# A longer hand-written order for ScalarE and VectorE through the gates of an mLSTM layer

## The chip, the cores and the metric

One Trainium2 chip, one of its cores. The metric is device time in microseconds (us) of one execution of the whole program; lower is better. TensorE multiplies matrices, ScalarE and VectorE work elementwise, GpSimd does small elementwise work, SyncE issues most of the transfers.

## The reference, cut to what matters

A decoder of two layers on 256 positions of width 1024, all in float32: an mLSTM mixer, a convolutional feed-forward net, an attention mixer and another feed-forward net. The change touches the mLSTM mixer:

```python
u = rmsnorm(x, norm_g) @ w_in
q, k, v, o, gi, gf = split(u)            # 4 heads; q, k 128 wide, v, o 256 wide
i_pre, f_pre = gi + b_gates[0], gf + b_gates[1]
lf = log_sigmoid(f_pre)                  # summed over the positions
...
s = (q @ k.T) * exp(decay)               # decay from the sums of lf, i_pre and a running maximum
h = s @ v / max(abs(sum(s)), exp(-m))
h = rmsnorm(h, h_norm_g) * sigmoid(o)
out = h @ w_out
```

## The kernel before, in words

Positions lie in two tiles of 128. TensorE does float32 products out of two rounded parts: every operand X is held as hi (X rounded, float32r) and lo (X minus hi). A weight *unit* is 128 x 2048 floats (1 MB): `unit` (L137) loads it into one of three `raw` buffers and splits it in two halves of 128 x 1024; for each half ScalarE writes hi (L144) and VectorE lo (L145), into one of four hi and four lo buffers.

The mLSTM layer (L429 to L634) has these stages for TensorE, in a written order that the change nearly keeps:

1. Gates (L525) and k, q (`kq_steps`, L516, products on L216 and L220): eight results kq0 to kq7 of 128 x 256, from units kq0 to kq3 of `w_kq`. Each result is evicted by `whole` (L253): a ScalarE copy (L257) and a VectorE addition (L258).
2. Among the steps of kq4 to kq7: the norm's sums (L185, L187, GpSimd L189 gives `rc`); `gates` (L453): two small products (L457), then VectorE L460 and L463, ScalarE Exp (L464), a table load and Ln (L465), VectorE `lf` (L466), the logarithm of the forget gate; `r.row` (L191) makes the row factor `rB` (L194, L196); `scale` (L520) multiplies each kq by `rB` (L521).
3. `sums_f` (L468): three small products with `lf` (L470 to L472), ScalarE `fc` (L473), GpSimd `av` (L474). Then four blocks of 16 steps over units vo0 to vo7 of `w_vo`, two units for each block; a step is three products of 512 columns (L237 to L239).
4. Block 1 (vo0, vo1): its results go to V (L572, L573); `maxima` (L476): transposes of `av`, VectorE L480, eight steps of a running maximum (L484), and the split into `mh`, `ml` (L488, by L150 and L151).
5. Block 2 (vo2, vo3): among its steps `decay` for four heads (products L500, L501 of `selr` with `mh` and `ml`; VectorE L503, L505; ScalarE Exp L507 into E), `floors` (transposes L493, VectorE L494 into `em`), and `scores` (L554, L555, then VectorE L556). These small results share three PSUM buffers named mis.

`mix(steps, items)` (L70) puts items among the steps by a running cost. TensorE's order is as written everywhere. For ScalarE and VectorE the order is as written only from L374 to `first.close()` on L544; from there a scheduler orders them by its own estimate of times, and units of weights that the written part does not hold back are placed where the scheduler finds an engine free. What a written instruction waits for holds up all that stands behind it on its engine.

Of the kernel before, what the change touches and what calls it, by code (L numbers as in the profile page):

```python
# [11 lines left out]
F32 = mybir.dt.float32  # L12
F32R = mybir.dt.float32r
BF16 = mybir.dt.bfloat16
AF = mybir.ActivationFunctionType
OP = mybir.AluOpType
AX = mybir.AxisListType

P = 128
# [6 lines left out]
MH = 4  # L26
# [43 lines left out]
def mix(steps, items=()):  # L70

    items, now = list(items), 0.0
    for cost, step in steps:
        while items and items[0][0] <= now:
            items.pop(0)[1]()
        step()
        now += cost
    for _, item in items:
        item()
# [3 lines left out]
def yoco_kernel(ctx: ExitStack, tc: tile.TileContext, A, out):  # L83
    nc = tc.nc
# [5 lines left out]
    wraw = ctx.enter_context(tc.tile_pool(name="wraw", bufs=3))  # L90
    wsp = ctx.enter_context(tc.tile_pool(name="wsp", bufs=4))
# [19 lines left out]
    for j in range(4):  # L111
        c = slice(j * 512, (j + 1) * 512)
# [24 lines left out]
    def unit(src, length, pieces=PIECES):  # L137
        raw = wraw.tile([P, 2048], F32, name="raw")[:, :length]
        nc.sync.dma_start(raw, src)
        hi = wsp.tile([P, 2048], F32R, name="hi")[:, :length]  # L140
        lo = wsp.tile([P, 2048], F32R, name="lo")[:, :length]
        for j in range(pieces):
            c = slice(j * length // pieces, (j + 1) * length // pieces)
            nc.scalar.activation(hi[:, c], raw[:, c], AF.Copy)  # L144
            nc.vector.tensor_tensor(lo[:, c], raw[:, c], hi[:, c].bitcast(F32), OP.subtract)  # L145
        return hi, lo

    def split(hi, lo, src, g=None):
        if g is None:
            nc.scalar.activation(hi, src, AF.Copy)  # L150
            nc.vector.tensor_tensor(lo, src, hi.bitcast(F32), OP.subtract)  # L151
        else:
            nc.scalar.activation(hi, src, AF.Copy, scale=g)
            nc.vector.scalar_tensor_tensor(lo, src, g, hi.bitcast(F32), op0=OP.mult, op1=OP.subtract)

# [84 lines left out]

        return [(0.64, lambda k=k: one(k)) for k in range(KD)]

    def block_x(src, first, x, done):

        u = [Once(lambda j=j: unit(src[first + j], 2048)) for j in range(2)]
        return [s for t in range(NT) for s in steps_x(t, u, x, done)]

    def acc():  # L250
# [122 lines left out]
    first = ExitStack()  # L373
# [55 lines left out]
    with tc.tile_pool(name="mls", bufs=1, reuse_waits="tile") as mp, \  # L429
# [1 line left out]
        r = Rstd()  # L431

        psg = acc()
        grow = []
        lf = mp.tile([P, NT, MH], F32, name="lf")
        gs = mp.tile([P, NT, 2 * MH], F32, name="gs")
        fc = mp.tile([P, NT, MH], F32, name="fc")
# [13 lines left out]
        E = [mp.tile([P, 384], F32, name=f"E{h}") for h in range(MH)]  # L451

        def gates():  # L453
            tc.keep_in_program_order(nc.scalar.activation(selr, sel, AF.Copy))
            pt = mis()
            for t in range(NT):
                nc.tensor.matmul(pt[:, t * 2 * MH:(t + 1) * 2 * MH], grow[0][:, t * P:(t + 1) * P], both8,  # L457
                                 start=True, stop=True)
            for t in range(NT):
                nc.vector.scalar_tensor_tensor(gs[:, t], pt[:, t * 2 * MH:(t + 1) * 2 * MH], r.rc[:, t:t + 1],  # L460
                                               row[:, R_G:R_G + 2 * MH], op0=OP.mult, op1=OP.add)
            fg = gs[:, :, MH:]
            nc.vector.scalar_tensor_tensor(lf, fg, -1.0, fg, op0=OP.mult, op1=OP.min)  # L463
            nc.scalar.activation(lf, lf, AF.Exp)  # L464
            nc.scalar.activation(lf, lf, AF.Ln, bias=1.0)  # L465
            nc.vector.scalar_tensor_tensor(lf, fg, 0.0, lf, op0=OP.min, op1=OP.subtract)  # L466

        def sums_f():  # L468
            pf = mis()
# [6 lines left out]
        def maxima():  # L476
            pa = mis()
            for t in range(NT):
                nc.tensor.transpose(pa[:MH, t * P:(t + 1) * P], av[:, t], ident)
            nc.vector.tensor_scalar(mx[0][:, P:], pa[:MH, :S], 0.0, None, op0=OP.max)  # L480
            src = 0
            for step in range(8):
                d = 1 << step
                nc.vector.tensor_tensor(mx[1 - src][:, P:], mx[src][:, P:],  # L484
                                        mx[src][:, P - d:P + S - d], OP.max)
                src = 1 - src

            split(mh[:MH], ml[:MH], mrow[:MH])  # L488

        def floors():  # L490
            pc = mis()
# [24 lines left out]
        def kq_steps(j):  # L516
            return steps_w(pk[j], wk[j // 2], lambda k: k * 256 + (j % 2) * P, setA, range(KD), KD,
                           lambda p: whole(p, kq[j]))

        def scale(j):  # L520
            nc.vector.tensor_tensor(kq[j], kq[j], r.rB, OP.mult)  # L521
# [17 lines left out]
        for k in range(3, KD):  # L539
            squares(k, nc.vector)  # L540
        mix(kq_steps(2)[1:] + kq_steps(3))
        mix([s for j in range(4, 2 * MH) for s in kq_steps(j)],
            [(2.3, r.sums), (2.4, wk[3]), (6.2, gates), (6.2, r.row), (10.0, sums_f)])
        first.close()  # L544
        for j in range(2 * MH):
            scale(j)


        PT = [[mp.tile([P, 384], F32R, name=f"PT{h}{j}") for j in range(2)] for h in range(MH)]
# [74 lines left out]
        def at(t0, dt, fn, args):  # L624
            return [(t0 + dt * i, lambda a=a: fn(*a)) for i, a in enumerate(args)]

        mix(block_x(A["w_vo"], 0, setA, v_done(0)), [(1.2, maxima)])
        nc.sync.dma_start(rope, A["rope"])
        mix(block_x(A["w_vo"], 2, setA, v_done(1)),
            at(1.8, 0.6, decay, [(h,) for h in range(MH)]) + [(4.2, floors)]  # L630
            + at(5.1, 1.2, scores, [(h,) for h in range(MH)]))
        mix(block_x(A["w_vo"], 4, setA, o_done(0)), at(0.9, 1.05, head, [(h, t) for h in range(MH) for t in range(NT)]))
# [202 lines left out]
```

## Time and profile before

| | us |
|---|---|
| median of 3 runs | 602.84 (601.43 to 603.41) |
| the profiled execution, its own time | 602.72 |
| its span in the trace | 601.0 |
| TensorE busy | 592.1 (99%) |
| VectorE, ScalarE, GpSimd busy | 484.8, 390.0, 159.2 |
| HBM read | 104.15 MB |

Times in the trace count from the start of the span; the program's own time is 1.7 us longer than the span. "Granted clock" is the share of TensorE's full clock that it was given: 1.0 is 2.4 GHz, 0.5 is 1.2 GHz. A row of a timeline with x6 is six instructions that follow each other; its length runs from the first one's start to the last one's end. A matmul is shown from its start to the end of its last column, which overlaps the next one, so the distance of two starts is its price in a stream.

### The profile page before, as it was taken

How to read it: one execution, taken by the hardware profiler on the slowest of the kernel's cores; microseconds unless marked ns; L12 is line 12 of the kernel's file. 1: busy time of each engine (PE TensorE's matmuls, PEld its weight loads, DVE VectorE, ACT ScalarE, POOL GpSimd, SP SyncE). 2: the span in 40 equal slices, each digit the busy share in tenths (PEclk: the TensorE clock that was granted, in tenths of full speed). 3: DMA queues.
4: the chain of work that ended last, by engine and by line, in shares of the span. 5: the costliest groups of instructions: out<-in, count | busy, mean ns of one | idle time of the engine just before them, and what ended most of it. 6: DMA issues, size and time to landing. Idle time of an engine off the chain costs nothing.

```text
span 601.0 us, 9385 instructions
## 1 busy us (share of the span) xinstructions
PE 592.1 (99%) x3506; PEld 518.6 (86%) x3506; DVE 484.8 (81%) x812; ACT 390.0 (65%) x711; POOL 159.2 (26%) x179
## 2 busy tenths in 40 slices
PE   8979999999999999999999999999999999999997
PEld 5868889998888888888888878899988888888887
DVE  6888676979999999988768786466999999998650
ACT  6746676757777777665556687555687767676430
POOL 3000410553544344301111200022454444432000
PEclk9979999999999999999999999999999999999999
DMA  8684343526454543485754533335345546346830
GB/s 284 252 310 152 147 140 141 208 75 251 168 186 166 198 137 139 144 269 198 251 206 178 200 122 134 138 142 210 121 169 201 183 169 209 102 141 202 273 109 17
DMA packets 18622, 105.80 MB, mean 176 GB/s; under 512 B 2320, under 2 KB 3856, under 8 KB 9104
## 3 DMA queue, kind: packets, MB, share of 16 engines
q1 hardware_dynamic: 18288, 104.68, 49.2%
q10 hardware_dynamic: 288, 0.52, 0.3%
q8 instruction: 27, 0.44, 0.3%
q14 instruction: 19, 0.16, 0.1%
HBM read 104.15 MB, written 1.05 MB: 175 GB/s over the span
## 4 chain that ended last, share of the span: by engine, by line
PE 96%; DMA 2%; ACT 1%; DVE 1%; SPq 0%; issue 0%
PE acc L216 38%; PE acc L220 24%; PE acc L213 10%; PE acc L237 6%; PE acc L239 6%; PE acc L238 6%; DMA hT<-xT 1%; DMA raw<-w_vo 1%; PE mis L587 1%; PE mis L703 1%; PE acc L715 1%; ACT hi L144 0%; PE mis L731 0%; PE acc L713 0%; DVE lo L145 0%; PE mis L745 0%
## 5 line engine op out<-in xcount | busy, mean ns | idle before, releaser
L145 DVE TENSOR_TENSOR lo<-raw,hi 128x1024 fp32r<-128x1024 f32 (+1 forms) x212 | 239.3, 1164 | 32.9 <-ACT hi L144 32.7
L144 ACT ACTIVATE hi<-raw 128x1024 fp32r<-128x1024 f32 (+1 forms) x212 | 195.2, 969 | 48.3 <-PE acc L216 20.2
L216 PE MATMUL acc<-xb,hi 128*128 128x512 f32 x608 | 207.6, 396 | 0.0
L220 PE MATMUL acc<-xb,lo 128*128 128x256 f32 x736 | 191.7, 280 | 0.0
L220 PEld LDWEIGHTS acc<-xb,lo 128*128 128x128 f32 x736 | 138.2, 189 | 6.7
L216 PEld LDWEIGHTS acc<-xb,hi 128*128 128x128 f32 x608 | 108.7, 188 | 20.6
L216 PE MATMUL acc<-f,hi 128*128 128x512 f32 x330 | 115.0, 394 | 0.0
L302 DVE SCALAR_TENSOR_TENSOR y<-whole,par,y 128x254 f32<-128x254 f32 (+1 forms) x176 | 109.9, 639 | 5.5 <-ACT y L299 5.0
L220 PE MATMUL acc<-f,lo 128*128 128x256 f32 x352 | 96.8, 282 | 0.0
L317 POOL TENSOR_TENSOR a<-sg,y 128x256 f32<-128x256 f32 x44 | 51.8, 1176 | 96.4 <-ACT sg L315 96.4
L299 ACT ACTIVATE y<-whole,par 128x256 f32<-128x256 f32 x88 | 52.1, 594 | 32.1 <-DVE whole L258 32.1
L216 PEld LDWEIGHTS acc<-f,hi 128*128 128x128 f32 x330 | 61.1, 188 | 13.0
L220 PEld LDWEIGHTS acc<-f,lo 128*128 128x128 f32 x352 | 66.1, 188 | 1.3
L319 POOL TENSOR_TENSOR f<-a,f 128x256 fp32r<-128x256 f32 x44 | 45.1, 1026 | 43.7 <-ACT f L318 43.7
L237 PE MATMUL acc<-hi,xa 128*128 128x512 f32 x128 | 54.2, 423 | 0.0
L239 PE MATMUL acc<-hi,xa 128*128 128x512 f32 x128 | 50.8, 397 | 0.0
L238 PE MATMUL acc<-lo,xa 128*128 128x512 f32 x128 | 50.7, 396 | 0.0
L172 POOL TENSOR_TENSOR sqacc<-sqacc,sq 128x256 f32<-128x256 f32 x18 | 18.4, 1024 | 108.3 <-ACT sq L171 108.2
L213 PE MATMUL acc<-xb,hi 128*128 128x256 f32 x256 | 45.4, 283 | 0.0
L220 PE MATMUL acc<-xa,lo 128*128 128x256 f32 x160 | 43.8, 286 | 0.5 <-DVE lo L151 0.5
L213 PEld LDWEIGHTS acc<-xb,hi 128*128 128x128 f32 x256 | 39.0, 191 | 0.2
L213 PE MATMUL acc<-xa,hi 128*128 128x256 f32 x192 | 34.6, 283 | 0.0
(188 smaller groups left out, 735.7 us busy)
## 6 DMA issues: line engine op xcount, KB each, us to landing
raw<-w_up SPq DMA_DIRECT2D x44, 1024.0 KB, 4.8
raw<-w_down SPq DMA_DIRECT2D x32, 704.0 KB, 4.2
raw<-w_kqv SPq DMA_DIRECT2D x12, 1024.0 KB, 4.8
raw<-w_vo SPq DMA_DIRECT2D x8, 1024.0 KB, 5.4
raw<-w_out SPq DMA_DIRECT2D x4, 1024.0 KB, 4.7
raw<-w_o SPq DMA_DIRECT2D x4, 1024.0 KB, 4.8
raw<-w_kq SPq DMA_DIRECT2D x2, 1024.0 KB, 8.1
raw<-w_kq SPq DMA_DIRECT2D x2, 512.0 KB, 6.7
```

The source lines that it names most:

```text
L144: nc.scalar.activation(hi[:, c], raw[:, c], AF.Copy)
L145: nc.vector.tensor_tensor(lo[:, c], raw[:, c], hi[:, c].bitcast(F32), OP.subtract)
L213: nc.tensor.matmul(p[:, :S], hi[:, c], xs[k], start=alone[0] and k == 0 and n == 0, stop=alone[1] and last and n == 1)
L216: nc.tensor.matmul(p, hi[:, c], both[k], start=k == 0, stop=last)
L220: nc.tensor.matmul(p[:, :S], lo[:, c], xh[k], start=False, stop=False)
L237: nc.tensor.matmul(p, xh[k][:, ts], hi[:, c], start=k == 0, stop=False)
L238: nc.tensor.matmul(p, xh[k][:, ts], lo[:, c], start=False, stop=False)
L239: nc.tensor.matmul(p, xl[k][:, ts], hi[:, c], start=False, stop=k == KD - 1)
L299: nc.scalar.activation(y, u, AF.Identity, bias=b, scale=w[2])
L302: nc.vector.scalar_tensor_tensor(y[:, d:], u[:, :S - d], w[j], y[:, d:], op0=OP.mult, op1=OP.add)
L317: nc.gpsimd.tensor_tensor(out=a, in0=sg, in1=y[0], op=OP.mult)
L319: nc.gpsimd.tensor_tensor(out=al[i], in0=a, in1=ah[i].bitcast(F32), op=OP.subtract)
```

## The change

The written order of ScalarE and VectorE goes on beyond the gates. Unit vo0 is split in two written halves: the first in `ahead`, before the gates, the second in `between`, after them. `rB` is made ahead of the gates, `lf` and the scaling are placed by hand, and `scale(6)`, `scale(7)` come before `first.close()`. Units vo1 to vo3 are made by `behind(marks, ...)`, which lets their instructions be issued only after the marked ones: vo1 after Ln and `lf`, vo2 and vo3 after `mh` and `ml`. The copy `selr` moves from the gates behind `mh` and `ml`. On TensorE `sums_f` moves from before block 1 to behind its first step, and the transposes of `av` from the second step to the fourth.

```diff
     def split(hi, lo, src, g=None):
...
+        return (nc.scalar.activation(hi, src, AF.Copy, scale=g),
+                nc.vector.scalar_tensor_tensor(lo, src, g, hi.bitcast(F32), op0=OP.mult, op1=OP.subtract))
+
+    def behind(marks, make):
+
+        with ExitStack() as st:
+            for m in marks:
+                st.enter_context(tc.issue_after(m.ins))
+            return make()
...
         def gates():
-            tc.keep_in_program_order(nc.scalar.activation(selr, sel, AF.Copy))
...
-            nc.scalar.activation(lf, lf, AF.Ln, bias=1.0)
-            nc.vector.scalar_tensor_tensor(lf, fg, 0.0, lf, op0=OP.min, op1=OP.subtract)
+            marks.append(nc.scalar.activation(lf, lf, AF.Ln, bias=1.0))
+
+        def log_f():
+            marks.append(nc.vector.scalar_tensor_tensor(lf, gs[:, :, MH:], 0.0, lf, op0=OP.min, op1=OP.subtract))
...
-            split(mh[:MH], ml[:MH], mrow[:MH])
+            marks[:] = split(mh[:MH], ml[:MH], mrow[:MH])
+            behind(marks, lambda: nc.scalar.activation(selr, sel, AF.Copy))
...
+        vo = [Once(lambda j=j: behind(marks, lambda: unit(A["w_vo"][j], 2048))) for j in range(4)]
+        rawv = wraw.tile([P, 2048], F32, name="raw")
+        v0 = [None, None]
+
+        def ahead():
+            wk[3]()
+            nc.sync.dma_start(rawv, A["w_vo"][0])
+            v0[:] = [wsp.tile([P, 2048], F32R, name=nm) for nm in ("hi", "lo")]
+            split(v0[0][:, :1024], v0[1][:, :1024], rawv[:, :1024])
+            vo[0].made = tuple(v0)
+
+        def between():
+            c = slice(1024, 2048)
+            r.row()
+            nc.scalar.activation(v0[0][:, c], rawv[:, c], AF.Copy)
+            gates()
+            for j in range(3):
+                scale(j)
+            nc.vector.tensor_tensor(v0[1][:, c], rawv[:, c], v0[0][:, c].bitcast(F32), OP.subtract)
+
+        def then():
+            log_f()
+            for j in range(3, 6):
+                scale(j)
+
         mix([s for j in range(4, 2 * MH) for s in kq_steps(j)],
-            [(2.3, r.sums), (2.4, wk[3]), (6.2, gates), (6.2, r.row), (10.0, sums_f)])
+            [(2.3, r.sums), (2.4, ahead), (5.4, between), (8.0, then)])
+        scale(6), scale(7)
         first.close()
-        for j in range(2 * MH):
-            scale(j)
+        vo[1]()
...
-        mix(block_x(A["w_vo"], 0, setA, v_done(0)), [(1.2, maxima)])
+        mix(block_x(A["w_vo"], 0, setA, v_done(0), vo[:2]), [(0.6, sums_f), (2.4, maxima)])
...
-        mix(block_x(A["w_vo"], 2, setA, v_done(1)),
+        mix(block_x(A["w_vo"], 2, setA, v_done(1), vo[2:]),
```

How the built programs stand on the engines, at the three places that matter. The number in a name tells instances apart (kq6_249 is the seventh result of kq).

ScalarE before, from the second half of stage 2 to `fc`; hi_395 is unit kq3, hi_510, hi_545, hi_595 and hi_628 are vo0, vo1, vo2 and vo3:

```order
L144 ACTIVATE hi_395<-raw_393 128x1024 x2
L144 ACTIVATE hi_510<-raw_508 128x1024 x2
L144 ACTIVATE hi_545<-raw_543 128x1024 x2
L257 ACTIVATE kq5_248<-acc_401 128x256
L454 ACTIVATE selr_236<-sel_196 128x512
L144 ACTIVATE hi_595<-raw_593 128x1024 x2
L464 ACTIVATE lf_225<-lf_225 128x8
L465 ACT_TABLE_LOAD
L465 ACTIVATE lf_225<-lf_225 128x8
L196 ACTIVATE rB_442<-mis_439 128x256
L257 ACTIVATE kq6_249<-acc_420 128x256
L257 ACTIVATE kq7_250<-acc_454 128x256
```

The same stretch of ScalarE in the changed program; hi_396 is kq3, hi_403 is vo0, hi_491 is vo1:

```order
L144 ACTIVATE hi_396<-raw_394 128x1024 x2
L150 ACTIVATE hi_403<-raw_367 128x1024
L263 ACTIVATE kq5_248<-acc_407 128x256
L202 ACTIVATE rB_432<-mis_429 128x256
L565 ACTIVATE hi_403<-raw_367 128x1024
L469 ACTIVATE lf_225<-lf_225 128x8
L470 ACT_TABLE_LOAD
L470 ACTIVATE lf_225<-lf_225 128x8
L144 ACTIVATE hi_491<-raw_489 128x1024 x2
L263 ACTIVATE kq6_249<-acc_426 128x256
L263 ACTIVATE kq7_250<-acc_463 128x256
L480 ACTIVATE fc_227<-mis_521 128x8
```

Ahead of Exp and Ln there is now one half of vo0 and `rB` behind kq5's copy, where three whole units and `selr` stood; the whole of vo1 stands between Ln and kq6's copy.

VectorE before, in the same stretch:

```order
L145 TENSOR_TENSOR lo_396<-raw_393,hi_395 128x1024 x2
L145 TENSOR_TENSOR lo_511<-raw_508,hi_510 128x1024 x2
L145 TENSOR_TENSOR lo_546<-raw_543,hi_545 128x1024 x2
L258 TENSOR_TENSOR kq5_248<-acc_401,kq5_248 128x256
L460 SCALAR_TENSOR_TENSOR gs_226<-mis_430,rc_391,row_81 128x8 x2
L463 SCALAR_TENSOR_TENSOR lf_225<-gs_226 128x8
L145 TENSOR_TENSOR lo_596<-raw_593,hi_595 128x1024 x2
L466 SCALAR_TENSOR_TENSOR lf_225<-gs_226,lf_225 128x8
```

And in the changed program:

```order
L145 TENSOR_TENSOR lo_397<-raw_394,hi_396 128x1024 x2
L151 TENSOR_TENSOR lo_404<-raw_367,hi_403 128x1024
L264 TENSOR_TENSOR kq5_248<-acc_407,kq5_248 128x256
L465 SCALAR_TENSOR_TENSOR gs_226<-mis_435,rc_392,row_81 128x8 x2
L468 SCALAR_TENSOR_TENSOR lf_225<-gs_226 128x8
L529 TENSOR_TENSOR kq0_243<-kq0_243,rB_432 128x256
L529 TENSOR_TENSOR kq1_244<-kq1_244,rB_432 128x256
L529 TENSOR_TENSOR kq2_245<-kq2_245,rB_432 128x256
L569 TENSOR_TENSOR lo_404<-raw_367,hi_403 128x1024
L264 TENSOR_TENSOR kq6_249<-acc_426,kq6_249 128x256
L473 SCALAR_TENSOR_TENSOR lf_225<-gs_226,lf_225 128x8
```

The gates' VectorE work is ahead of all but three of the halves that preceded it, and `lf` (L473) stands behind kq6's addition, which needs kq6's copy on ScalarE.

VectorE in the changed program from the last maxima into block 2; lo_596, lo_629 and lo_719 are vo2, vo3 and vo4:

```order
L491 TENSOR_TENSOR mx0_230<-mx1_231 4x256
L151 TENSOR_TENSOR ml_235<-mx0_230,mh_234 4x256
L145 TENSOR_TENSOR lo_596<-raw_593,hi_595 128x1024 x2
L145 TENSOR_TENSOR lo_629<-raw_626,hi_628 128x1024 x2
L511 SCALAR_TENSOR_TENSOR E0_239<-mis_611,av_228,cmask_204 128x256
L513 SCALAR_TENSOR_TENSOR E0_239<-mis_611,av_228,cmask_204 128x128
L145 TENSOR_TENSOR lo_719<-raw_716,hi_718 128x1024
L511 SCALAR_TENSOR_TENSOR E1_240<-mis_620,av_228,cmask_204 128x256
L513 SCALAR_TENSOR_TENSOR E1_240<-mis_620,av_228,cmask_204 128x128
L145 TENSOR_TENSOR lo_719<-raw_716,hi_718 128x1024
L511 SCALAR_TENSOR_TENSOR E2_241<-mis_637,av_228,cmask_204 128x256
L513 SCALAR_TENSOR_TENSOR E2_241<-mis_637,av_228,cmask_204 128x128
```

Units vo2 and vo3, which stood ahead of the maxima, now stand behind them and ahead of the decays.

## Rows read from the trace of the kernel before

**Rows 1.** The page: busy us and share of the span, granted clock in 40 slices.
```profile
PE 592.1 (99%) x3506; PEld 518.6 (86%) x3506; DVE 484.8 (81%) x812; ACT 390.0 (65%) x711; POOL 159.2 (26%) x179
...
PEclk9979999999999999999999999999999999999999
```
**Rows 2.** Waits of TensorE over the whole span: total us, times, longest.
```profile
PE mis L470 <- DVE lf L466: 3.3, 1, 3.3
PE mis L131 <- DVE warm L125: 1.2, 1, 1.2
```
**Rows 3.** Timeline of TensorE at the wait: start, us, what, [idle before].
```profile
27.14 0.40 PE L220 MATMUL acc<-xa,lo 128*128 128x256 f32 x2
...
32.87 0.40 PE L216 MATMUL acc<-xa,hi 128*128 128x512 f32 x1
36.56 0.56 PE L470 MATMUL mis<-lf,tri 128*128 128x4 f32 x2 [3.29 <-DVE lf L466]
...
37.83 0.77 PE L237 MATMUL acc<-hi,xa 128*128 128x512 f32 x1
```
**Rows 4.** Stretches: length, busy us (instructions) by engine, granted clock, DMA share, GB/s.
```profile
36.00:38.00 2.00, 1.44 (x7) 1.47 (x8) 1.69 (x7) 1.99 (x6) 0.00 (x0) 0.50 0.91 274
38.00:40.00 2.00, 2.00 (x5) 1.61 (x6) 2.00 (x5) 0.99 (x2) 0.20 (x1) 0.50 1.01 426
...
42.00:44.00 2.00, 2.00 (x9) 1.58 (x8) 1.71 (x5) 0.00 (x0) 0.00 (x0) 0.82 0.60 160
```
**Rows 5.** Timeline of ScalarE around the gates.
```profile
23.88 0.38 ACT L257 ACTIVATE kq<-acc 128x256 f32<-128x256 f32 x1 [1.46 <-PE acc L216]
24.16 5.79 ACT L144 ACTIVATE hi<-raw 128x1024 fp32r<-128x1024 f32 x6
...
30.11 0.62 ACT L454 ACTIVATE selr<-sel 128x512 fp32r<-128x512 f32 x1
32.59 2.00 ACT L144 ACTIVATE hi<-raw 128x1024 fp32r<-128x1024 f32 x2 [1.86 <-DMA raw<-w_vo]
34.51 0.19 ACT L464 ACTIVATE lf<-lf 128x8 f32<-128x8 f32 x1
34.71 1.28 ACT L465 ACT_TABLE_LOAD   x1
36.01 0.21 ACT L465 ACTIVATE lf<-lf 128x8 f32<-128x8 f32 x1
```
**Rows 6.** Timeline of VectorE around the gates and in the maxima.
```profile
25.24 6.90 DVE L145 TENSOR_TENSOR lo<-raw,hi 128x1024 fp32r<-128x1024 f32 x6 [0.46 <-ACT hi L144]
32.06 0.41 DVE L258 TENSOR_TENSOR kq<-acc,kq 128x256 f32<-128x256 f32 x1
32.40 0.35 DVE L460 SCALAR_TENSOR_TENSOR gs<-mis,rc,row 128x8 f32<-128x8 f32 x2
...
36.25 0.17 DVE L466 SCALAR_TENSOR_TENSOR lf<-gs,lf 128x8 f32<-128x8 f32 x1 [0.20 <-ACT lf L465]
36.52 1.43 DVE L521 TENSOR_TENSOR kq<-kq,rB 128x256 f32<-128x256 f32 x4
...
42.48 1.30 DVE L484 TENSOR_TENSOR mx<-mx 4x256 f32<-4x256 f32 x3
```
**Rows 7.** Timeline of VectorE in block 2.
```profile
52.54 0.73 DVE L573 SCALAR_TENSOR_TENSOR V<-acc,rc,V 128x512 fp32r<-128x512 f32 x1
53.23 1.23 DVE L145 TENSOR_TENSOR lo<-raw,hi 128x1024 fp32r<-128x1024 f32 x1
54.37 0.48 DVE L503 SCALAR_TENSOR_TENSOR E<-mis,av,cmask 128x256 f32<-128x256 f32 x1
...
55.02 1.22 DVE L145 TENSOR_TENSOR lo<-raw,hi 128x1024 fp32r<-128x1024 f32 x1
```
**Rows 8.** Timeline of TensorE at full clock, two matmuls of block 1, 34 apart.
```profile
44.10 0.39 PE L238 MATMUL acc<-lo,xa 128*128 128x512 f32 x1
...
51.81 0.39 PE L239 MATMUL acc<-hi,xa 128*128 128x512 f32 x1
```

More of the change, by code (lines that the diff above doesn't have):

```diff
@@ L149, in split @@
         if g is None:
[L150 to L154, printed above, removed]
+            return (nc.scalar.activation(hi, src, AF.Copy),
+                    nc.vector.tensor_tensor(lo, src, hi.bitcast(F32), OP.subtract))
+        return (nc.scalar.activation(hi, src, AF.Copy, scale=g),
[5 more added lines that the diff above has]
+            return make()
     def operand(pool, name, n):
@@ L243, in steps_x, with block_x @@
         return [(0.64, lambda k=k: one(k)) for k in range(KD)]
-    def block_x(src, first, x, done):
-        u = [Once(lambda j=j: unit(src[first + j], 2048)) for j in range(2)]
+    def block_x(src, first, x, done, u=None):
+        u = u or [Once(lambda j=j: unit(src[first + j], 2048)) for j in range(2)]
         return [s for t in range(NT) for s in steps_x(t, u, x, done)]
@@ L433, in yoco_kernel @@
         psg = acc()
-        grow = []
+        grow, marks = [], []
         lf = mp.tile([P, NT, MH], F32, name="lf")
```

## The prediction

> **What bounds the kernel now.** The page comes first: TensorE is busy for 99% of the span and was granted its full clock but for one place, the third of 40 slices [rows 1]. So only what makes TensorE idle or slow counts, and the other engines matter where it waits for them. TensorE's waits, longest in total first, name one long one after the start: 3.3 us for `lf` on VectorE; no other reaches 1.2 us [rows 2]. In the timeline kq7's last product starts at 32.87, the first product with `lf` at 36.56, after 3.29 us idle [rows 3]. Then the stretches: granted clock 0.50 from 36 to 42 (two rows alike, one shown) and 0.82 from 42 to 44 [rows 4], so TensorE comes back at 1.2 GHz, having run at 2.4 until it stopped. The timelines of ScalarE and VectorE say why `lf` is late: ScalarE converts three whole units in 5.79 us, does kq5's copy and `selr`, waits for vo2's load, converts vo2 in 2.00 us, and only then does Exp, the table load and Ln [rows 5]; VectorE subtracts for six halves in 6.90 us before kq5's addition and the gates [rows 6].
>
> **What the change removes.** In a stream of products (price below) the next one could have gone 0.23 us after 32.87, at 33.1; it went at 36.56, so 3.46 us are lost, the row's 3.29 and the tail of the last product [rows 3]. The lost clock is half a microsecond for each at 0.50: from 36.56 to 42 that is 2.72 us, and 42 to 44 lacks 0.18 of 2 us, 0.36 us. Together 3.08 us. If nothing new came, 6.54 us would go. No instruction is added; transposes, copies and transfers are the same in number, so only order is priced.
>
> **Prices, start to start.** ScalarE: a hi half (5.79 - 1.05)/5 = 0.95 us, taking the last as some 1.05 long; a copy 23.88 to 24.16, 0.28; `selr` some 0.55 of its 0.62 [rows 5]. VectorE: a lo half (6.90 - 1.2)/5 = 1.14; an addition 32.06 to 32.40, 0.34; a scaling (1.43 - 0.41)/3 = 0.34; a maximum step (1.30 - 0.42)/2 = 0.44 [rows 6]; a pair of decay operations 54.37 to 55.02, 0.65; a V subtraction 0.69 [rows 7]. TensorE: a 512-column product (51.81 - 44.10)/34 = 0.227, so a step 0.68 [rows 8]; `sums_f` took 1.27 us at half clock [rows 3, 4], 0.64 at full. From VectorE's end of `lf` (36.25 + 0.17) to TensorE's start at 36.56 is 0.14 us [rows 3, 6]; I add it to every handover to TensorE.
>
> **The sums, new place.** Until 25 us both orders are alike. ScalarE: kq3 at 24.16 and 25.11, vo0's first half to 27.1; kq5's copy when TensorE ends kq5 (27.14 [rows 3]), to 27.5; `rB` and vo0's second half, to 29.0. VectorE: halves of kq3 from 25.24, vo0's first half to 28.7, kq5's addition, the gates (two at 0.35, one more at 0.17), to 29.55. So Exp goes at 29.6, not 34.51; with the table load's 1.28 and Ln's 0.21 the end is 31.2 [rows 5]. Now vo1 stands in front: two hi halves to 33.0, then kq6's copy to 33.4. VectorE, which holds `lf` behind kq6's addition, adds to 33.8 and ends `lf` at 33.95. TensorE ends kq7 at 33.1 and has the first step of block 1 (0.68), to 33.8; vo0 is ready. It starts the sums at 33.95 + 0.14 = 34.1: **0.3 us** idle in place of 3.29, at full clock. `rB` and the three scalings on VectorE ahead of this are covered: kq6's addition can't start before 33.4, and they end at 31.8 with vo0's second half.
>
> **Block 1** then has 45 products at 0.227, the sums' 0.64 and two transposes at some 0.07: from 34.1 to 45.1. vo1's lo halves: three scalings after 33.95 to 35.0, the halves to 36.1 and 37.25. TensorE wants the first after seven more products and the sums, at 36.9. Covered, by 0.8 us.
>
> **Block 2, the new queue.** VectorE from 37.25: kq7's addition, two scalings and the first maximum, 4 x 0.34, to 38.6; five maximum steps, 2.2; V's subtraction, 0.69; three steps, 1.3: to 42.8. ScalarE does `mh` (0.3) and `selr` (0.55), to 43.65, and only now vo2: first hi half to 44.7, lo half on VectorE to 45.9. TensorE is there at 45.1, does one product with hi and needs lo at 45.3; it gets it at 46.05: **0.75 us**. VectorE then has three more halves (to 49.3), E of head 0 (49.95), half of vo4 (51.1), E1 (51.75), half (52.9), E2 (53.55). TensorE runs the rest of step 1 (0.46) and two steps to 47.9, then four times a decay (0.24) and a step, to 51.6. The transposes of `floors` need the mis buffer that E1 frees: 51.9, **0.3 us**; a step later, at 52.75, the scores of head 0 need the buffer of E2: 53.7, **0.95 us**. Later scores come 1.9 us apart and E3 is out by 54.9, so TensorE is ahead no more. From there everything is as before, shifted; the loads that wait for a raw buffer start later, vo5's most: when vo2's lo halves end, at 47.0, some 14 us before block 3.
>
> **Sum.** 6.54 - 0.3 - 0.75 - 0.3 - 0.95 = 4.24 us. Against the profiled execution's 602.72 this gives **598.5 us**; that execution lies 0.12 below the median of the three, 602.84, which I disregard. A measurement of this kernel tells a change from none at about 0.3%, 1.8 us.
>
> **Unknown prices and bounds.** A short wait of TensorE is priced by 0 (covered) below and by its own length with the 0.14 handover above; each of the four can shift by the length of what is queued before it, at most one half (1.14). I take the computed values, since they rest on rows of the same instructions. Whether several short waits within 9 us lower the clock no row shows: at best nothing, at worst one more loss like 3.08. I take nothing, as the only fall came with 3.29 us without a product.
>
> A rule against this: the Trainium skill (ScalarE: Activation LUTs, What ACT_TABLE_LOAD costs) puts a table switch at about 2.66 us, a drain included. Here the load is 1.28 us, begins 0.01 after Exp's end and Ln follows 0.02 after it [rows 5]; the trace disagrees, and I keep 1.28. By the page `lf` would end about 1.4 us later, the sums' wait would be 1.7, and the sum would give some 599.9 us.
>
> **Rivals.**
> - *The later waits are covered.* If VectorE's chain through the maxima runs some 1 us shorter, or V's subtraction comes late enough to let the maxima pass, most of 2.0 us of waiting in block 2 goes: 602.72 - 6.54 + 0.3 = 596.5. Against it: the prices are measured in that very chain.
> - *The clock falls again in block 2.* Three waits of 0.3 to 0.95 in 45 to 54, with little time between the last two. Price, the same loss as now: 598.5 + 3.1 = 601.6. The Trainium skill (TensorE: Matmul & The Clock Gate, A second HAM failure mode: psum-queue depth-cycling) says that short idling between groups of products, repeated, can make the clock swing. No stretch of this trace has such a pattern, so it neither agrees nor disagrees.
> - *`lf` is held behind vo1 (slower).* The mechanism is one in-order chain: kq6's addition waits for kq6's copy, which waits for vo1's conversion. If vo1's conversion starts 2.5 us later than I have it (its load or Ln late), `lf` ends at 36.4, TensorE idles for some 2.8 us, near the 3.29 that brought the clock down, and nearly the whole 6.54 comes back while the 2.0 us of block 2 stay: 602.72 + 2.0 = 604.7, over the bound of 604.65. It decides from some 2.5 us of delay; a smaller one costs its own length. For it: vo1 is a whole unit, 1.9 us of ScalarE. Against: before, vo1's conversion ran without a gap from its predecessors by 29.95 [rows 5], so its data were there.
> - *It doesn't do what it says.* The scheduler still orders all behind `first.close()`; if it undid the gain by another placement, the time would stay at 602.7. The built order shows `lf` early, so this has little.
>
> **How the numbers follow.** Forecast 0.70, covered waits 0.09, clock 0.11, slower 0.05, no change 0.05. The forecast's own range, with each of two waits half a lo half (0.57) either way and a little for runs that differ, is 597.0 to 600.0. Eight in ten: down to the covered case less 0.2, 596.3; up into a clock that falls for most of its price, 601.2. Faster by over 0.3% (below 601.0) is the forecast, the covered case and a shorter fall of the clock, 0.70 + 0.09 + 0.05 = 0.84; within 0.3% 0.11; slower 0.05.
>
> **What would show it.** Right: TensorE's wait for `lf` below 1 us and PEclk at 9 in the third slice; Exp near 29.6; a wait of some 0.75 us on a product with vo2's lo near 46; waits of some 0.3 and 0.95 at the transposes of `floors` and the first scores, each for VectorE; block 3 some 4 us earlier. Wrong: a wait at the sums above 1.5 us, granted clock below 1 between 33 and 60, or a new wait past 60 us, where I price nothing.

## The result, and the profile after

| | before | changed |
|---|---|---|
| median of five executions, us | 602.21 (601.43 to 603.41) | 599.25 (598.47 to 599.65) |
| ratio, 95% interval | | 0.9945 (0.9929 to 0.9961) |
| the profiled execution, its own time, us | 602.72 | 599.65 |
| its span, us | 601.0 | 597.9 |
| mean granted clock of its span | 0.994 | 1.000 |

The change is faster by some 0.55%. The forecast, 598.5 us with a range of 596.3 to 601.2, named the right side, and the time lies in the range, 0.75 us above the forecast.

The granted clock by slice, from the page of the changed kernel (before: [rows 1]):

```profile
PEclk9999999999999999999999999999999999999999
```

The dip in the third slice is gone. TensorE's waits over the whole span, without the two at the very start (engine, what, releaser: total us, times, longest; before: [rows 2]):

```profile
PE mis L588 <- DVE E L513: 0.6, 1, 0.6
PE acc L244 <- DVE lo L145: 0.4, 1, 0.4
```

The wait of 3.3 us for `lf` is no longer there; in its place stand 0.6 us at the first scores (L588 now) and 0.4 us at the first product with vo2's lo half (L244). Lines lie six or more further down than before. TensorE's timeline shows the four places at which the prediction expected a wait (start us, us, what, [idle before]; before: [rows 3, 8]):

```profile
24.66 0.39 PE L191 MATMUL mis<-tri,sqacc 128*128 128x1 f32 x3
...
34.68 0.40 PE L245 MATMUL acc<-hi,xa 128*128 128x512 f32 x1
35.12 0.36 PE L477 MATMUL mis<-lf,tri 128*128 128x4 f32 x2
...
46.30 0.39 PE L243 MATMUL acc<-hi,xa 128*128 128x512 f32 x1
47.05 0.50 PE L244 MATMUL acc<-lo,xa 128*128 128x512 f32 x1 [0.36 <-DVE lo L145]
47.39 0.40 PE L245 MATMUL acc<-hi,xa 128*128 128x512 f32 x1
...
52.53 0.40 PE L245 MATMUL acc<-hi,xa 128*128 128x512 f32 x1
52.89 0.44 PE L501 MATMUL mis<-ident,mx 128*128 128x128 f32 x2
53.09 0.48 PE L243 MATMUL acc<-hi,xa 128*128 128x512 f32 x1
...
53.64 0.40 PE L245 MATMUL acc<-hi,xa 128*128 128x512 f32 x1
54.68 0.70 PE L588 MATMUL mis<-kq,kq 128*128 128x256 f32 x2 [0.64 <-DVE E L513]
55.21 0.38 PE L589 MATMUL mis<-kq,kq 128*128 128x128 f32 x2
...
90.19 0.28 PE L219 MATMUL acc<-xb,hi 128*128 128x256 f32 x1
```

Idle time understates these waits, since a row's length covers the tail of a product. Start to start is fairer. In a stream the next product starts 0.227 us later [rows 8]. At the sums (34.68 to 35.12) 0.44 - 0.23 = 0.21 us are lost though no idle time is noted; where `lf` is long done, as in experiment 2, the same step takes 0.23 (36.29 to 36.52). At vo2's lo half 0.75 - 0.23 = 0.52 are lost, and 0.34 - 0.23 = 0.11 more at the restart: 0.63 us. For the last two places the run without waits, shown further down, is the measure (there 0.23 and 0.14 around the transposes of `floors`, 0.23 and 0.43 around the scores): `floors` 0.13 + 0.06 = 0.19, scores 0.81 + 0.10 = 0.91 us. Together **1.94 us**.

ScalarE in the changed kernel, around the gates and ahead of vo2 (before: [rows 5]):

```profile
30.55 0.21 ACT L469 ACTIVATE lf<-lf 128x8 f32<-128x8 f32 x1 [0.53 <-DVE lf L468]
30.78 1.28 ACT L470 ACT_TABLE_LOAD   x1
32.08 0.21 ACT L470 ACTIVATE lf<-lf 128x8 f32<-128x8 f32 x1
32.19 1.99 ACT L144 ACTIVATE hi<-raw 128x1024 fp32r<-128x1024 f32 x2
...
43.85 0.42 ACT L150 ACTIVATE mh<-mx 4x256 fp32r<-4x256 f32 x1 [2.03 <-DVE mx L491]
44.17 0.61 ACT L496 ACTIVATE selr<-sel 128x512 fp32r<-128x512 f32 x1
44.69 5.79 ACT L144 ACTIVATE hi<-raw 128x1024 fp32r<-128x1024 f32 x6
```

VectorE in the same stretch (before: [rows 6, 7]):

```profile
34.48 0.42 DVE L264 TENSOR_TENSOR kq<-acc,kq 128x256 f32<-128x256 f32 x1 [1.82 <-ACT kq L263]
34.82 0.16 DVE L473 SCALAR_TENSOR_TENSOR lf<-gs,lf 128x8 f32<-128x8 f32 x1
...
45.77 4.63 DVE L145 TENSOR_TENSOR lo<-raw,hi 128x1024 fp32r<-128x1024 f32 x4 [1.05 <-ACT hi L144]
50.32 0.47 DVE L511 SCALAR_TENSOR_TENSOR E<-mis,av,cmask 128x256 f32<-128x256 f32 x1
```

The order is the one forecast: Exp, table load and Ln ahead of vo1's hi halves; `lf` behind kq6's addition; `mh` and `selr` when the maxima are done, and only behind these vo2's halves.

**Where the time went.** Two products stand at the same place of TensorE's order in every kernel here: the first of the norm's sums (A, `mis<-tri,sqacc`) and the first product of the output projection (B, `acc<-xb,hi`). All that the change moves lies between. In the profile of before they are

```profile
23.68 0.28 PE L185 MATMUL mis<-tri,sqacc 128*128 128x1 f32 x2
...
93.25 0.28 PE L213 MATMUL acc<-xb,hi 128*128 128x256 f32 x1
```

so before took 69.57 us from A to B and the changed kernel 65.53 (24.66 to 90.19 above), **4.04 us less**. The part from B to the end lasts 507.7 us in both. The part up to A, where both orders are alike, was 0.98 us longer in the changed kernel's profile. Hence 602.72 - 4.04 + 0.98 = 599.66, the profiled 599.65. Whether this 0.98 us belongs to the change is asked below. The table holds these three parts for the one profile of each kernel:

| kernel | to A | A to B | B to end of span |
|---|---|---|---|
| before, first profile | 23.68 | 69.57 | 507.7 |
| before, second and third | 24.61, 24.32 | 69.76, 68.19 | 507.7, 507.8 |
| changed, first and second profile | 24.66, 25.14 | 65.53, 65.48 | 507.7, 507.7 |
| before, clock kept up | 24.65 | 67.22 | 507.8 |
| before, sums later | 23.68 | 70.54 | 507.7 |
| changed, vo2 and vo3 not held | 23.83 | 71.30 | 507.7 |
| changed, vo1 not held | 23.51 | 65.50 | 507.7 |
| changed, sums at the old place | 23.48 | 65.73 | 507.7 |
| changed, fourth small buffer | 23.47 | 64.37 | 510.6 |
| changed, one decay in a large buffer | 24.37 | 64.84 | 507.7 |
| changed, all later waits out | 24.29 | 63.76 | 507.7 |

### The profile page after: what moved, and what is told of

Its sections match the earlier page's. It is cut to its first block, busy times and chain, and to the rows that moved or that the text cites. A ratio compares the mean times of both kernels' runs of the same rounds, so it can differ in the third digit from the quotient of the medians.

```text
span 597.9 us, 9386 instructions
## 1 busy us (share of the span) xinstructions
PE 591.7 (99%) x3506; PEld 517.7 (87%) x3506; DVE 484.8 (81%) x812; ACT 389.8 (65%) x711; POOL 159.1 (27%) x179
## 3 DMA queue, kind: packets, MB, share of 16 engines
HBM read 104.15 MB, written 1.05 MB: 176 GB/s over the span
## 4 chain that ended last, share of the span: by engine, by line
PE 96%; DVE 2%; DMA 1%; ACT 0%; issue 0%; SPq 0%; ACTq 0%; DVEq 0%
PE acc L222 39%; PE acc L226 25%; PE acc L219 10%; PE acc L243 6%; PE acc L245 6%; PE acc L244 5%; DVE lo L145 1%; PE mis L621 1%; DMA fst<-first 1%; PE mis L737 1%; PE acc L749 1%; PE mis L765 0%; PE acc L747 0%; PE acc L533 0%; PE mis L588 0%
## 5 line engine op out<-in xcount | busy, mean ns | idle before, releaser
L144 ACT ACTIVATE hi<-raw 128x1024 fp32r<-128x1024 f32 (+1 forms) x210 | 193.1, 968 | 46.1 <-PE acc L222 20.3
L243 PE MATMUL acc<-hi,xa 128*128 128x512 f32 x128 | 53.2, 415 | 0.0
L244 PE MATMUL acc<-lo,xa 128*128 128x512 f32 x128 | 50.1, 392 | 0.4 <-DVE lo L145 0.4
L245 PE MATMUL acc<-hi,xa 128*128 128x512 f32 x128 | 50.2, 392 | 0.0
```

The source lines that it names most:

```text
L243: nc.tensor.matmul(p, xh[k][:, ts], hi[:, c], start=k == 0, stop=False)
L244: nc.tensor.matmul(p, xh[k][:, ts], lo[:, c], start=False, stop=False)
L245: nc.tensor.matmul(p, xl[k][:, ts], hi[:, c], start=False, stop=k == KD - 1)
```

## The experiments

Theory: before lost its time once at the sums, half of it as idle time and half through the clock that fell in it; the changed order ends both, and what it hands on are short waits that each cost their length. Rivals: the clock is the whole matter and the idle time would be lost elsewhere anyway; or the early `lf` alone makes the gain and the held units are of no use.

**1. The clock alone.** Before, with products on zeros in the gap:

```diff
         def sums_f():
+            ps = mis()
+            for j in range(12):
+                nc.tensor.matmul(ps, warm[:, :P], warm, start=True, stop=True)
             pf = mis()
```

> The kernel before with 12 dummy products of 512 columns on TensorE between kq7 and the sums, where it idled; nothing else is changed. Theory (the loss was 3.46 us of idle plus 3.08 us of half clock, and the clock fell because TensorE had no products): lf still ends near 36.4 and the sums still start near 36.6, but at a granted clock of 1.0, so the time falls by about 3 us, to some 599.2, as much as the whole change gave. Rival (the clock falls for another cause, such as the transfers that fill the DMA engines there, at a share of 1.0 from 34 to 40): granted clock 0.5 near 36 to 42 again and no gain, 602.2.

Ratio to before 0.997 (0.9958 to 0.9981), 600.7 against 602.76 us: 2.1 us less, where some 3 were expected. The granted clock is 1.00 through the stretch, A to B 2.35 us shorter. The DMA share stays at 1.01 and 1.04 from 34 to 38 us, so the transfers, which the rival blamed, do not lower the clock. TensorE's rows:

```profile
37.34 0.39 PE L473 MATMUL mis<-lf,tri 128*128 128x4 f32 x2 [0.50 <-DVE lf L466]
...
39.27 0.40 PE L239 MATMUL acc<-hi,xa 128*128 128x512 f32 x1
40.20 0.38 PE L482 MATMUL mis<-ident,av 128*4 128x128 f32 x2 [0.53 <-POOL av L477]
```

The sums start nearly where they did, counted from A (12.69 us behind it, before 36.56 - 23.68 = 12.88). A new wait takes back 0.93 - 0.23 = 0.70 us, start to start (39.27 to 40.20): at full clock TensorE comes to the transposes of `av` before GpSimd has written it. So the clock alone is 2.35 - 0.19 + 0.70 = 2.86 us. Kept up by itself it gives 2.35 of the change's 4.04 us; for the rest the idle time has to go too.

**2. The sums later, the rest as before.** The order of before, with `sums_f` five steps into block 1 and the maxima behind it:

```diff
-            [(2.3, r.sums), (2.4, wk[3]), (6.2, gates), (6.2, r.row), (10.0, sums_f)])
+            [(2.3, r.sums), (2.4, wk[3]), (6.2, gates), (6.2, r.row)])
...
-        mix(block_x(A["w_vo"], 0, setA, v_done(0)), [(1.2, maxima)])
+        mix(block_x(A["w_vo"], 0, setA, v_done(0)), [(3.2, sums_f), (4.8, maxima)])
```

> The kernel before with only TensorE's part of the change, carried further: the sums go behind five steps of block 1 and the transposes of av behind the eighth; ScalarE and VectorE stay with the scheduler. Theory (the written order of ScalarE and VectorE is needed, since the maxima and mh come late behind the halves of units): the idle before the sums goes, since vo0 and vo1 are split by 32, but block 2 then waits for mh and ml at the first decay, some 5 us, with the clock falling; the time stays or rises, 602 to 604. Rival (the idle was only a matter of where TensorE has its sums): no wait above 1 us and 596 to 599.

Ratio 1.0022 (1.0009 to 1.0035). The wait at the sums is gone, and TensorE pays more for the next thing in the chain:

```profile
51.80 0.58 PE L500 MATMUL mis<-mh,selr 128*128 128x256 f32 x1 [4.68 <-ACT mh L150]
```

The clock falls behind this wait too: it is granted 0.50 from 52 to 56 us. On VectorE four lo halves, of vo4 and vo5 by the order of the units, stand among the maxima (42.02 to 51.30), at 43.79, 45.26, 47.39 and 48.86:

```profile
43.79 1.21 DVE L145 TENSOR_TENSOR lo<-raw,hi 128x1024 fp32r<-128x1024 f32 x1
```

At 1.14 us each they are 4.6 us, about as much as the wait. So it is not enough that TensorE reaches the sums later: `lf`, sums, `av`, maxima, `mh`, decays are one chain over four engines, and it has to start earlier or to be kept free of these halves. Which of the two would do was not tried: no run holds the units back with `lf` as late as before and the sums later, so that the early `lf` is needed is not shown.

**3. The hold on vo2 and vo3 taken away.**

```diff
-        mix(block_x(A["w_vo"], 2, setA, v_done(1), vo[2:]),
+        mix(block_x(A["w_vo"], 2, setA, v_done(1)),
```

> The changed kernel without the holding of vo2 and vo3 behind mh and ml; vo1 stays held. In its built order three units and two halves then stand among the maxima on VectorE, and mh stands behind vo2 to vo5 on ScalarE. Theory (the later waits are the price of a queue that must stay so): the wait at vo2's lo half (0.36 us idle) goes, but TensorE waits some 6 us for mh and selr at the first decay, the clock falls, and the time is some 604 to 605, above the kernel before. Rival (the holding is what costs the 0.36 and 0.64 us of waits in block 2, and is not needed): 598.3.

Ratio to before 1.0026 (1.0014 to 1.0038): the whole gain is lost, and a little more. Here `lf` is as early as in the changed kernel (the sums start 10.47 us behind A in both), but the scheduler puts six lo halves, of vo3 to vo5 by the order of the units, between the first maximum (40.30) and `mh`, where the changed kernel has none; vo2's stand just ahead of them. The hold on vo2 and vo3 thus keeps vo4 and vo5 back as well. VectorE, then TensorE:

```profile
46.03 1.21 DVE L145 TENSOR_TENSOR lo<-raw,hi 128x1024 fp32r<-128x1024 f32 x1
...
47.83 0.40 DVE L491 TENSOR_TENSOR mx<-mx 4x256 f32<-4x256 f32 x1
48.16 2.34 DVE L145 TENSOR_TENSOR lo<-raw,hi 128x1024 fp32r<-128x1024 f32 x2
```

```profile
53.20 0.58 PE L508 MATMUL mis<-mh,selr 128*128 128x256 f32 x1 [5.43 <-ACT selr L496]
```

The split of the maxima, `mh`, begins at 52.21 (in the changed kernel at 43.85), 9.2 us later counted from A. TensorE waits 5.43 us and its clock falls again, to 0.50 from 52 to 56 us. The rival that the early `lf` alone makes the gain is refuted.

**4. The hold on vo1 taken away.**

```diff
+        vo[1] = Once(lambda: unit(A["w_vo"][1], 2048))
         vo[1]()
```

> The changed kernel without the hold on the second value unit (its copies and lo halves may come as soon as their loads and the order of the code let them; they then stand ahead of the gates' exponential on both engines); the holds on units 2 and 3 stay. Theory (what the holds are worth is worth in units 2 and 3 alone): the log of the gates comes some 0.7 us later, so TensorE waits 0.6 to 0.9 us at the sums, block 2's wait at the third unit's lo half (0.36 us) shrinks to under 0.25 us, since everything behind the second unit is done earlier: within 0.6 us of the changed kernel, either way. Rival (the hold on this unit is what keeps the gates early): the sums wait over 2.5 us and the clock falls again, 3 us slower or more.

598.61 us, ratio 0.9941 (0.9925 to 0.9958); A to B 65.50, as in the changed kernel. `lf` comes 0.38 us later against A and TensorE waits 0.42 us at the sums, less than the 0.6 to 0.9 expected; the wait at vo2's lo half is gone, the one at the scores is as it was. The hold that earns something is that on vo2 and vo3.

**5. A fourth small PSUM buffer** (`mis` 3 to 4, the large ones 5 to 4):

```diff
-    pacc = ctx.enter_context(tc.tile_pool(name="pacc", bufs=5, ...
-    pmis = ctx.enter_context(tc.tile_pool(name="pmis", bufs=3, ...
+    pacc = ctx.enter_context(tc.tile_pool(name="pacc", bufs=4, ...
+    pmis = ctx.enter_context(tc.tile_pool(name="pmis", bufs=4, ...
```

> The changed kernel with four small PSUM buffers (mis) and four large ones in place of three and five. Theory (TensorE waits at the first scores for a buffer that E2's operations free, not for E's values): the wait of 0.64 us at the scores goes and none takes its place, the wait at vo2's lo stays, and the time falls by about 0.8 to 1.3 us, to 598.2. Rival (VectorE itself is late in block 2, and TensorE meets it a step later anyway): the wait comes back at the heads or the next block and the time stays at 599.2; or the missing large buffer makes waits in the feed-forward stages and it is slower.

600.84 us, ratio 0.9972 (0.9961 to 0.9983): slower than the changed kernel. From A to B it wins 1.16 us, since the waits at `floors` and the scores are gone. From B on it loses 2.9, in the feed-forward stages, which now lack a large buffer:

```profile
PE acc L222 <- DVE whole L264: 1.1, 4, 0.3
```

This is the loss that the expectation named as a rival. The four waits on the eviction of a result are 1.1 us of idle time. Laid beside the changed kernel product by product, counted from B, each of the four costs 0.5 to 0.6 us (near 214, 226, 510 and 522 us), and two more places, near 203 and 499 us, cost 0.3 each without noted idle time: 2.8 of the 2.9 us.

**6. The same without that loss.** Only the fourth decay takes a large buffer, at a place where one is free:

```diff
-            mb = mis()[:, :S]
+            mb = (acc if h == 3 else mis)()[:, :S]
```

> The changed kernel, with the fourth decay's product in one of the five large PSUM buffers instead of one of the three small ones, for this one use, so that the feed-forward stages keep their five. Theory (each of the later waits costs its own length and no more): the wait of 0.64 us at the first scores goes, with the 0.16 us that a restarted row of products loses: 0.6 to 0.9 us less than the changed kernel, and the feed-forward stages, unlike in the run with four and four buffers, lose nothing (no waits of 0.26 us at 214, 226, 510, 522 us). Rival (VectorE's queue is the limit, the buffer only shows it): the scores' results or the first heads wait instead, under 0.3 us less.

598.61 us, ratio 0.9936 (0.992 to 0.9951), beside 599.15, 0.9946 (0.993 to 0.9962), for the changed kernel on the same chip:

> The changed kernel itself, as the reference of the three runs beside it. Both theories: ratio to the kernel before 0.993 to 0.996 (about 599.2 us); waits of TensorE at the first product with the third value unit's lo half 0.36 us and at the first scores 0.64 us. If the start of the whole run (when TensorE's clock first rises) differs from run to run, the lead over the kernel before at 24 us differs with it, and the lead won between 24 and 90 us stays 4.0 us.

The medians' difference of 0.54 us is within the spread of either. In the stretch it is plainer: A to B 64.84 against 65.53 and 65.48, 0.64 to 0.69 us less, no wait at the scores, and the feed-forward stages unchanged. This is the theory's 0.6 to 0.9; `floors` and scores had cost 1.10, so some 0.4 us come back as small delays further on.

**7. The sums back at their old place**, TensorE there half a microsecond earlier:

```diff
-        mix(..., vo[:2]), [(0.6, sums_f), (2.4, maxima)])
+        mix(..., vo[:2]), [(0.0, sums_f), (1.2, maxima)])
```

> The changed kernel with the gate sums and the maxima back at the places that they had in the order before (sums ahead of the first value block, maxima at 1.2 us of it), the rest as changed. Theory: the sums now come some 0.5 us before VectorE has written the log of the gates (34.98 us against TensorE at about 34.5), so TensorE waits 0.4 to 0.7 us there, and the wait at the third unit's lo half (0.36 us) shrinks by as much, since what it waits for doesn't move: within 0.4 us of the changed kernel, at most 0.4 slower. Rival (the two waits add up): 0.5 to 0.8 us slower.

598.73 us, ratio 0.9939 (0.9923 to 0.9955); A to B 65.73, 0.2 us more than the changed kernel. TensorE now waits for `lf`:

```profile
33.95 0.36 PE L477 MATMUL mis<-lf,tri 128*128 128x4 f32 x2 [0.74 <-DVE lf L473]
```

and the wait at vo2's lo half is gone. The two do not add up: TensorE is held back at one or at the other, because what it waits for in the end, the last of the chain, comes no sooner.

**8. All later waits out.** `selr` and vo2's hi halves are put behind `fc`, where ScalarE was idle, vo2's lo halves right behind `ml` on VectorE, and vo4 and vo5 behind the last decay:

```diff
-            nc.scalar.activation(fc..., AF.Copy)
+            m = [nc.scalar.activation(fc..., AF.Copy)]
+            behind(m, lambda: nc.scalar.activation(selr, sel, AF.Copy))
+            raw2 = wraw.tile([P, 2048], F32, name="raw")
+            nc.sync.dma_start(raw2, A["w_vo"][2])
+            v2[:] = [wsp.tile([P, 2048], F32R, name=nm) for nm in ("hi", "lo")] + [raw2]
+            for j in range(2):
+                c = slice(j * 1024, (j + 1) * 1024)
+                m.append(behind(m, lambda: nc.scalar.activation(v2[0][:, c], raw2[:, c], AF.Copy)))
...
-            behind(marks, lambda: nc.scalar.activation(selr, sel, AF.Copy))
+            for j in range(2):
+                c = slice(j * 1024, (j + 1) * 1024)
+                marks.append(behind(marks, lambda: nc.vector.tensor_tensor(
+                    v2[1][:, c], v2[2][:, c], v2[0][:, c].bitcast(F32), OP.subtract)))
+            vo[2].made = tuple(v2[:2])
...
+        vo[4:] = [Once(lambda j=j: behind(dm, lambda: unit(A["w_vo"][j], 2048))) for j in (4, 5)]
```

(`dm` holds the last decay's second operation; block 3 takes vo4 and vo5 from this list.)

> The changed kernel with the places of three things changed on ScalarE and VectorE: the copy of the selector and the two hi halves of the third value unit come right behind the copy of the gate sums (ahead of the split of the maxima), its lo halves right behind the lo part of the maxima, and the units of the third value block behind the last decay. Theory: neither the wait at the third unit's lo half (0.36 us) nor that at the first scores (0.64 us) is left, and with 0.16 us for each restart the kernel is 1.0 to 1.6 us faster than the changed one. Rival: the decays are held up behind the lo halves on VectorE, TensorE waits at the first decay for 1.5 to 2 us, and it is as fast as the changed kernel or up to 0.5 us slower.

597.06 us, ratio 0.9911 (0.9896 to 0.9927), the fastest kernel of the study: every one of its six executions (596.47 to 597.90) lies below the lowest of the changed kernel's on the same chip (598.38). TensorE's waits:

```profile
PE mis L131 <- DVE warm L125: 1.2, 1, 1.2
PE acc L226 <- DVE lo L151: 0.9, 2, 0.6
PE acc L222 <- DVE xa L153: 0.4, 1, 0.4
```

All three lie ahead of A. ScalarE and VectorE in block 1 and 2 of this run:

```profile
35.67 0.62 ACT L481 ACTIVATE selr<-sel 128x512 fp32r<-128x512 f32 x1
36.19 1.99 ACT L487 ACTIVATE hi<-raw 128x1024 fp32r<-128x1024 f32 x2
```

```profile
44.35 2.34 DVE L505 TENSOR_TENSOR lo<-raw,hi 128x1024 fp32r<-128x1024 f32 x2
46.62 2.34 DVE L145 TENSOR_TENSOR lo<-raw,hi 128x1024 fp32r<-128x1024 f32 x2
```

and TensorE at the transposes of `floors` (L512) and the scores (L600, L601), without a wait, as used above:

```profile
51.55 0.39 PE L245 MATMUL acc<-hi,xa 128*128 128x512 f32 x1
51.78 0.38 PE L512 MATMUL mis<-ident,mx 128*128 128x128 f32 x2
51.92 0.48 PE L243 MATMUL acc<-hi,xa 128*128 128x512 f32 x1
...
52.46 0.39 PE L245 MATMUL acc<-hi,xa 128*128 128x512 f32 x1
52.69 0.59 PE L600 MATMUL mis<-kq,kq 128*128 128x256 f32 x2
53.12 0.39 PE L601 MATMUL mis<-kq,kq 128*128 128x128 f32 x2
```

vo2's first lo half begins at 44.35 (in the changed kernel at 45.77), 1.05 us sooner counted from A, and between the decays no half of vo4 stands any more. A to B is 63.76 us, 1.77 less than in the changed kernel. The three waits behind the sums had cost 0.63 + 0.19 + 0.91 = 1.73 us by the rows: the account closes, a little above the 1.0 to 1.6 expected, which had priced `floors` at nothing and a restart at 0.16.

**9. Before, profiled twice more.** Two things had to be settled: the late start, and how far before's single profile stands for its executions.

> The kernel before, for another profile of its start. If the later start of the changed kernels' profiles (0.0 to 1.5 us at 24 us of the span, against the one profile of before) is chance, this start lies anywhere in that spread, and the stretch from 24 to 90 us takes as long as in the first profile, within 0.3 us. If it comes from the change, the start stands within 0.2 us of the first profile's, and so does that of the next run.

> The kernel before once more, with the same two expectations as the run ahead of it: the start somewhere between 0.25 us earlier and 1.5 us later than in the first profile (chance), or within 0.2 us of it (the change). The idle stretch at the gate sums 3.1 to 3.5 us and the clock at half for 6.83 us behind it in either case.

A came at 24.61 and 24.32 in these, 0.93 and 0.64 us later than in the first profile of the same kernel, and over all thirteen profiles it lies between 23.47 and 25.14, without regard to the kernel. So the start does not come from the change, and before's first profile, 23.68, caught an early one. The idle time at the sums was 3.18 and 3.17 us, as expected. The clock was not. Windows (length, busy us of five engines, granted clock, DMA share, GB/s) of the second profile, then of the third:

```profile
36.00:38.00 2.00, 0.59 (x4) 0.62 (x5) 1.69 (x4) 1.99 (x6) 0.00 (x0) 0.92 0.92 352
38.00:40.00 2.00, 2.00 (x7) 1.71 (x8) 2.00 (x7) 1.84 (x3) 0.09 (x1) 0.50 0.82 303
...
44.00:46.00 2.00, 2.00 (x9) 1.58 (x9) 0.58 (x2) 0.00 (x0) 0.00 (x0) 0.87 0.88 369
```

```profile
38.00:40.00 2.00, 2.00 (x7) 1.17 (x7) 2.00 (x7) 1.54 (x3) 0.20 (x1) 0.63 0.77 315
40.00:42.00 2.00, 2.00 (x8) 1.57 (x6) 2.00 (x2) 0.00 (x0) 0.00 (x0) 0.51 0.36 152
```

In the second the clock is at half for 2 x 0.08 + 3 x 1.00 + 2 x 0.13 = 3.4 us of lost full-clock time, that is for 6.8 us (40 to 44, left out, is at 0.50), as in the first profile. In the third only these two windows are below 1.00; 2 x (0.37 + 0.49) = 1.7 us are lacking, half as much, and A to B is 1.4 to 1.6 us shorter. That is a miss: 6.83 us at half clock and a stretch within 0.3 us of the first profile's were expected in either case.

## Why the prediction was right

*What bounds the kernel, and what is removed: right.* The wait for `lf` and the half clock both went, and the experiment with the clock alone (2.86 us of clock once products fill the gap) shows that they are two losses of one cause.

*The places: right to a few hundredths.* Counted from A, the changed profile runs 0.98 us behind the first one of before. Less this, Exp is at 29.57 (forecast 29.6), the sums at 34.14 (34.1), vo2's lo half is taken at 46.07 (46.05), `floors` at 51.91 (51.9), the first scores at 53.70 (53.7). Orders of instructions and durations of the same instructions elsewhere in the trace were enough for this.

*The sizes: the waits and the saving a little too long, and two places priced at nothing.* The four waits cost 0.21, 0.63, 0.19 and 0.91 us against 0.3, 0.75, 0.3 and 0.95, 1.94 together instead of 2.30. The clock's part was priced at half of the time at 0.50. A product of 512 columns there took 0.43 us and not twice 0.227, as before's timeline has it:

```profile
39.26 0.63 PE L237 MATMUL acc<-hi,xa 128*128 128x512 f32 x1
39.69 0.63 PE L238 MATMUL acc<-lo,xa 128*128 128x512 f32 x1
```

So 47% of the 6.16 us at half clock (2 x 3.08) are lost, 2.9 and not 3.08; the run with the clock alone gave 2.86. Priced at nothing were 0.13 us from A to the last product of kq7 (9.32 us in the changed kernel, 9.19 before) and 0.20 us from the second scores to B (33.37, before 33.17). From A to B this makes 4.24 + 0.36 - 0.18 - 0.13 - 0.20 = 4.09 us, measured 4.04. That the four errors nearly cancel is luck. It is no luck that a wait is shorter when TensorE comes late to it: a wait ends when VectorE is done, and at vo2's lo half TensorE came some 0.25 us later than thought, and lost 0.52 us ahead of the product, not 0.75. Up to the scores the last release alone counts, and the run with the sums at their old place shows it: 0.74 us of waiting at the sums, and 0.2 us in the result.

*Two readings on the way were off, without effect.* By the prediction's own rows Ln ends at 29.6 + 1.71 = 31.3 (34.51 to 36.22 in [rows 5]), not 31.2; measured, less 0.98, 31.31. And vo1's lo half is wanted after nine more products, not seven; its 36.9 is what nine give.

*The base: the larger part of the 0.75 us.* The sum was made against one profiled execution, 602.72, and its distance to the median was disregarded. That execution had a start some 0.5 us earlier than the mean of the other twelve profiles (24.2). Counting this back, 602.72 - 4.04 + 0.5 = 599.2 is within 0.1 us of the median measured. That this one execution lies near before's median is chance: of the 57 executions of before that are listed beside the experiments with their mean granted clock, 37 had 0.993 or 0.994 and a median of 603.0, 20 had 0.997 and a median of 601.5. The profile used stood for the first kind only. Against the second kind the change is worth some 2.3 us (601.5 - 599.2).

*The rivals.* The clock did not fall in block 2: it is granted 1.0 from 34 to 56 with waits of 0.36 and 0.64 us in that stretch, so 601.6 did not come. The Trainium skill (TensorE: Matmul & The Clock Gate, A second HAM failure mode: psum-queue depth-cycling) had been the page for that rival; two such waits 7.6 us apart are no case of the repeated pattern that it describes, and the trace neither confirms nor refutes it. The covered waits (596.5) did not come; with all of them taken out, in experiment 8, the time was 597.06. `lf` held up behind vo1 did not happen either; with vo1 let go ahead of Exp, `lf` came 0.38 us later. The slower case has a neighbour that the text did not name: the units behind vo1 getting in among the maxima, 604.45 us when vo2 and vo3 are set free.

*The table load.* The Trainium skill (ScalarE: Activation LUTs, What ACT_TABLE_LOAD costs) puts a switch at about 2.66 us with its drain. Here the load took 1.28 us again, began at 30.78, 0.02 behind Exp's end, and Ln followed 0.02 behind it; the measurement decides, and the row was the right price.

## What to carry to other kernels

When a wait is removed, follow the chain behind it to its last release: the time won ends there, and waits ahead of it in the same chain replace each other rather than add up. An order written further is worth what it keeps out of that chain (here six halves of vo3 to vo5 among the maxima, some 6.8 us at 1.14 each), so hold back first what isn't urgent but can get in between. And profile the kernel before more than once: split the span at products that the change doesn't move, so that a late start or a shorter fall of the clock is not taken for part of the change.

## What the runs showed of the hardware

With the same order, the clock's fall behind an idle stretch of TensorE of some 3.2 us lasted 6.8 us twice and 3.4 us once. When it came differed as well: in the first profile the clock was at half when the products started again [rows 3, 4]; in the second the first rows behind the wait were still at full pace; in the third it fell a microsecond or more after the start, with TensorE busy. So one loss has two prices, 1.5 us apart, and the same kernel shows two groups of times.

The changed kernel has such a fall of its own, at another place. Its second profile, with the latest A of all (25.14), shows 1.79 us without products ahead of the first product with weights at 7.15, and behind it a granted clock of 0.58 and 0.57 from 8 to 12 us. In before's third profile 1.73 us at the same place left the clock at 1.00. The later waits of 0.36 to 0.74 us left it at 1.00 in every profile here.

The start of the span is not fixed either: the same instructions up to A took between 23.47 and 25.14 us.
